# Sparse attention of a decoder trunk: query blocks 0 and 1 become one unit, and VectorE adds the causal mask in PSUM

## Chip, cores and metric

The kernel runs on one core of a Trainium2 chip, in one launch. The metric is the device time of one execution in microseconds (us), lower is better. Engines are named as in the profile: PE (TensorE matmuls), PEld (its weight loads), DVE (VectorE), ACT (ScalarE), POOL (GpSimd), SP (SyncE).

## What is computed

Two layers of a decoder trunk on 512 tokens of width 1024. Each layer runs two token mixers on the same normalised input, stick-breaking attention and native sparse attention (NSA), multiplies each by a SiLU path, projects both up, merges them by sigmoid gates, projects once more and adds the input. The change is in the NSA part:

```python
def masked_softmax(s, mask):
    return jax.nn.softmax(jnp.where(mask, s.astype(jnp.float32), NEG_INF), axis=-1)
...
        ss = jnp.einsum('bgrqd,bgqkd->bgrqk', qb, ks) * scale
        ps = masked_softmax(ss, (tok <= tq[:, None])[:, :, None])
        o_s = jnp.einsum('bgrqk,bgqkd->bgrqd', ps.astype(vs.dtype), vs)
...
        sw = jnp.einsum('bgrqd,bgkd->bgrqk', qb, kw) * scale
        pw = masked_softmax(sw, mw)
        o_w = jnp.einsum('bgrqk,bgkd->bgrqd', pw.astype(vw.dtype), vw)
```

There are 8 query heads in 2 key groups. With 512 tokens, 8 selected blocks of 64 and a window of 512, the selected branch and the window branch both attend to all earlier tokens, so both reduce to causal attention over key blocks of 128 tokens, with different keys and values. Query block i (0 to 3) attends to key blocks 0 to i, and only its last key block needs the triangular mask.

## The kernel before

**Stages of a layer.** Stage X does the stick-breaking attention (lines 1101 to 1185), stage Y the NSA attention (lines 1186 to 1218), and then come the gates, the up projection and the output projection (from line 1220). All large products are float32 split into a high and a low part of a rounded format, three products each (`gemm`, line 436): a projection of 128 columns is 24 matmuls of 512 columns into a bank of tag `acc`, of which there are two.

**Order of the work.** The order of PE's instructions is that of the Python code (line 75). The queues of DVE, ACT and POOL are filled by the framework, by priority and program order, and each engine then runs its queue in order. PE's order is paced by a planner, the class `Pacer` (line 304): every matmul adds its planned time to a clock (0.216 us for 512 columns). Projections wait in a list as filler, and `pump(us)` issues filler matmuls until the clock has moved on by so much, or the filler is empty. So a latency of other engines is covered with projections. In stage Y the filler is what is left of the query projections, then the SiLU paths `z` and the first 13 of 16 gate projections `g` (`Y_FILL`, line 523); what the loop doesn't use is issued by `pc.drain()` (line 1218).

**Stage Y.** For each of 4 head pairs j (one head from each key group g) and each query block i there is a unit u, 16 in all, and each does these steps:

- `nsa_qk` (line 1024): scores into PSUM banks of tag `S` (four banks), at most two key blocks to a bank, both branches t side by side. For each bank and g there is a product with the low part of the keys, kN2, on 64 rows of the array (the two g on different halves), and one with the stacked high parts, kN1, on 128 rows. Units 0 and 1 have one bank for each g, units 2 and 3 have two. Then line 1047 adds the mask of the last key block by a bfloat16 product of `mk_n` with the identity, 256 columns, once for each g.
- Softmax: DVE takes the maximum of each bank (line 1052; over two banks also line 1054), ACT the exponentials with their sums (line 1057), DVE the reciprocal times the branch's gate (lines 1061 and 1062) and the scaling of the probabilities `pr` (line 1065). `pr` has tag `P`, five buffers, two of them for a unit; the SiLU paths use the same tag.
- `nsa_t` (line 1068): four transposes for each key block into the one bank of tag `tp`, a copy by ACT (line 1078), and a pump of `Y_GAP` = 1.5.
- `nsa_pv` (line 1083): 8 products of 128 columns for each key block, on 64 columns of the array, into the bank `o`.

The loop (lines 1193 to 1217) is software-pipelined: `pump(ready - now)`, the products `nsa_pv` of unit u-1, then `nsa_qk` of unit u+1, which sets `ready` to the clock plus `Y_LAT` of that unit, then `nsa_t` of unit u. With a head pair's first unit come `cmp_t` and `cmp_pv` of the compressed branch, whose scores `cmp_qk` (line 980) makes in the pair before (for the first pair, just ahead of the loop):

```python
                    pc.pump(ready - pc.now)
...
                        nsa_pv(o, pTs, (u - 1) % NT)
...
                        pr[u + 1] = nsa_qk(j2, (u + 1) % NT)
                        ready = pc.now + Y_LAT[(u + 1) % NT]
...
                    pTs = nsa_t(pr.pop(u), i, Y_GAP)
```

Of the kernel before, what the change touches and what calls it, by code (L numbers as in the profile page):

```python
# [13 lines left out]
F32 = mybir.dt.float32  # L14
F32R = mybir.dt.float32r
BF16 = mybir.dt.bfloat16
I32 = mybir.dt.int32
AF = mybir.ActivationFunctionType
ALU = mybir.AluOpType
AX = mybir.AxisListType  # L20
PSUM = bass.MemoryType.PSUM

P = 128
# [3 lines left out]
NT = S // P  # L27
# [8 lines left out]
NEG = -1e30  # L36
# [7 lines left out]
X_GAP = (3.5, 3.4)  # L44
Y_GAP = 1.5
F_GAP = ((6.0, 8.0), (5.0, 7.0))
Y_LAT = (7.3, 6.9, 6.9, 8.8)
N_GATE = 13


# [1 line left out]
def kernel(  # L52
# [20 lines left out]
    V, A, T, G = nc.vector, nc.scalar, nc.tensor, nc.gpsimd  # L73

    ctx.enter_context(tc.manual_schedule(engines={mybir.EngineType.PE}))
    cp = ctx.enter_context(tc.tile_pool(name="cp", bufs=1))
# [5 lines left out]
    wk = ctx.enter_context(tc.tile_pool(name="wk", bufs=6))  # L82
# [9 lines left out]
    def s_bank():  # L92
        return bank("S", 4)
# [15 lines left out]
                            bass.AP(tensor=positions.tensor, offset=positions.offset, ap=[[16, NCMP], [1, 32]]))  # L109
    identf = cp.tile([P, P], F32, name="identf")  # L110
    make_identity(nc, identf)
    identb = cp.tile([P, P], BF16, name="identb")
    V.tensor_copy(identb, identf)
    onesf = cp.tile([P, P], F32, name="onesf")
    V.memset(onesf, 1.0)
    eps_t = cp.tile([P, 1], F32, name="eps_t")
# [33 lines left out]
    lns, exps, sigs = deque(maxlen=10), deque(maxlen=10), deque(maxlen=2)  # L150
# [21 lines left out]
    G.affine_select(scr, onesf, pattern=[[-1, P]], compare_op=ALU.is_ge, fill=0.0, base=0, channel_multiplier=1)  # L172
    ntri = cp.tile([P, P], F32R, name="ntri")
    V.tensor_scalar(ntri, scr, -1.0, None, op0=ALU.mult)
    zero = wk.tile([P, P], F32, tag="wk", name="zero")
    V.memset(zero, 0.0)
    mk_sb = cp.tile([P, P], F32, name="mk_sb")
    V.memset(mk_sb, -NEG)
    G.affine_select(mk_sb, mk_sb, pattern=[[1, P]], compare_op=ALU.is_gt, fill=NEG, base=0, channel_multiplier=-1)
    mk_n = cp.tile([P, 2, P], BF16, name="mk_n")  # L180
    mtmp2 = wk.tile([P, P], F32, tag="wk", name="mtmp2")
    G.affine_select(mtmp2, zero, pattern=[[-1, P]], compare_op=ALU.is_ge, fill=NEG, base=0, channel_multiplier=1)
    for b in range(2):
        V.tensor_copy(mk_n[:, b], mtmp2)
    mk_c = cp.tile([P, NT, 32], F32, name="mk_c")
    V.memset(mk_c, 0.0)
    for i in range(NT):
# [159 lines left out]
    pc = Pacer()  # L347

    def mm(out, lhsT, rhs, start, stop, us, **kw):
        T.matmul(out, lhsT, rhs, start=start, stop=stop, **kw)  # L350
        pc.tick(us)

    def tr(out, in_, ident):
        T.transpose(out, in_, ident)  # L354
        pc.tick(0.11)
# [287 lines left out]
    for l in range(depth):  # L643
# [3 lines left out]
        with ExitStack() as lc:  # L647
# [370 lines left out]
                       skip_group_check=True)  # L1018
                return o

            def n_halves(i):
                return [(0, min(2, i + 1))] + ([(2, i + 1)] if i > 1 else [])

            def nsa_qk(j, i):
                nX = n_in[j]
                qs = slice(i * P, (i + 1) * P)
                nk = i + 1
                halves = n_halves(i)
                nh = len(halves)
                pr = [py.tile([P, NT, 2, P], F32, tag="P", name="pr", bufs=5) for _ in range(2)]  # L1030
                mx = py.tile([P, 2, 2, 2], F32, tag="mx", name="mx", bufs=3)
                dn = py.tile([P, 2, 2, 2], F32, tag="dn", name="dn", bufs=3)
                rc = py.tile([P, 2, 2], F32, tag="rc", name="rc", bufs=3)
                sb = [[s_bank() for _ in halves] for _ in range(2)]
                for hf, (a, b) in enumerate(halves):
                    w = (b - a) * 256
                    for g in range(2):
                        gs = slice(g * HD, (g + 1) * HD)
                        mm(sb[g][hf][:, :w], nX[gs, g, qs], kN2[gs, a:b].rearrange("p k t c -> p (k t c)"),
                           True, False, w * .00022)  # L1040
                for hf, (a, b) in enumerate(halves):
                    w = (b - a) * 256
                    for g in range(2):
                        mm(sb[g][hf][:, :w], nX[:, g, qs], kN1[g][:, a:b].rearrange("p k t c -> p (k t c)"),
                           False, b < nk, w * .00043)
                for g in range(2):
                    mm(sb[g][-1][:, w - 256:w], identb, mk_n.rearrange("p t c -> p (t c)"), False, True, 0.11)
                for g in range(2):
                    sbk = []
                    for hf, (a, b) in enumerate(halves):  # L1050
                        sbk.append(sb[g][hf][:, :(b - a) * 256].rearrange("p (k t c) -> p t k c", t=2, c=P))
                        V.tensor_reduce(mx[:, hf, g], sbk[-1], axis=AX.XY, op=ALU.max, negate=True)  # L1052
                    if nh == 2:
                        V.tensor_tensor(mx[:, 0, g], mx[:, 0, g], mx[:, 1, g], op=ALU.min)
                    for hf, (a, b) in enumerate(halves):
                        for t in range(2):
                            exps.append(A.activation(pr[g][:, a:b, t], sbk[hf][:, t], AF.Exp,  # L1057
                                                     bias=mx[:, 0, g, t:t + 1], accum_out=dn[:, hf, g, t:t + 1]))
                    if nh == 2:
                        V.tensor_add(dn[:, 0, g], dn[:, 0, g], dn[:, 1, g])  # L1060
                    V.reciprocal(rc[:, g], dn[:, 0, g])
                    V.tensor_mul(rc[:, g], rc[:, g],
                                 vN[:, i, 264:280].rearrange("p (t g r) -> p t g r", t=2, g=2)[:, :, g, j])
                    for t in range(2):
                        V.tensor_scalar(pr[g][:, :nk, t], pr[g][:, :nk, t], rc[:, g, t:t + 1], None, op0=ALU.mult)  # L1065
                return pr

            def nsa_t(pr, i, gap):
                pTs = []
                for kb in range(i + 1):  # L1070
                    pt = t_bank()
                    ptv = pt.rearrange("p (g t q) -> p g t q", g=2, t=2)
                    for g in range(2):
                        for t in range(2):
                            tr(ptv[:, g, t], pr[g][:, kb, t], identf)
                    pT = py.tile([P, 2, 2, P], F32, tag="pT", name="pT", bufs=NT)
                    with tc.high_priority(offset=PRIO_SB):
                        A.activation(pT.rearrange("p g t q -> p (g t q)"), pt, AF.Copy)  # L1078
                    pTs.append(pT)
                    pc.pump(gap)  # L1080
                return pTs

            def nsa_pv(o, pTs, i):
                qs = slice(i * P, (i + 1) * P)
                for kb, pT in enumerate(pTs):
                    for t in range(2):
                        for g in range(2):
                            mm(o[g * HD:(g + 1) * HD, qs], vN[:, kb, t * P + g * HD:t * P + (g + 1) * HD],
                               pT[:, g, t], False, kb == i and t == 1, 0.115, skip_group_check=True)
# [96 lines left out]
            with ExitStack() as ly:  # L1186
                py = ly.enter_context(tc.tile_pool(name=f"py{l}", bufs=1, reuse_waits="tile"))
                pc.fill.extend([fills[kind](a) for kind, a in Y_FILL])
                sc = cmp_qk(0)
                pr = {0: nsa_qk(0, 0)}  # L1190
                ready = pc.now + Y_LAT[0]
                o, pTs = None, None
                for u in range(17):
                    j, i = u // NT, u % NT
                    pc.pump(ready - pc.now)
                    if i == 0 and u < 16:
                        pcT = cmp_t(sc)
                    if u > 0:
                        nsa_pv(o, pTs, (u - 1) % NT)
                        if i == 0:  # L1200
                            nsa_o(j - 1, o)
                    if u == 16:
                        break
                    if u < 15:
                        j2 = (u + 1) // NT
                        pc.until(lambda: j2 in n_in)
                        pr[u + 1] = nsa_qk(j2, (u + 1) % NT)
                        ready = pc.now + Y_LAT[(u + 1) % NT]
                        if i == 2 and j < 2:
                            pc.until(lambda: ("q", j + 2) in done)  # L1210
                            set_nX(j + 2, n_q[j + 2])
                    pTs = nsa_t(pr.pop(u), i, Y_GAP)
                    if i == 0:
                        o = cmp_pv(pcT)
                    if i == 2 and j < 3:
                        pc.until(lambda: j + 1 in n_in)
                        sc = cmp_qk(j + 1)
                pc.drain()
# [109 lines left out]
```

## Time and profile before

| what | value |
|---|---|
| median of 3 runs | 1007.01 us (1006.08 to 1008.62) |
| the profiled execution's own time | 1005.86 us |
| its span, first to last instruction | 1004.1 us |
| granted PE clock, mean of the span | 0.997 of full speed |
| PE, PEld, DVE, ACT busy | 97%, 77%, 68%, 47% |
| stage Y, layer 0 and layer 1 | about 218 to 408 us, about 701 to 890 us |

How to read it: matmuls are pipelined, and one that lasts 0.39 us can start 0.23 us after the one before it. So what a matmul costs PE is read from start to start in the timeline, not from its duration. In the timeline, a line is a run of like instructions: start, length, engine, line of the code, output and inputs, shapes, count, and in brackets the idle time before it and what ended that. L350 and L354 are the helpers `mm` and `tr`, so PE's work is told apart by its tiles.

### The profile page before, as it was taken

To read this page: it belongs to the slowest core of one execution; us is meant where nothing else is said; L and a number is where in the kernel's file an instruction comes from. 1 tells how busy PE (TensorE), PEld (TensorE's weight loads), DVE (VectorE), ACT (ScalarE), POOL (GpSimd) and SP (SyncE) were. 2 spreads that over 40 slices of the span, in tenths; PEclk is the share of its full clock that TensorE was granted. 3 is DMA by queue.
4 is the path that set the end of the run, shared out by engine and by line. 5 is a ranking of instruction groups with operands and counts; after the bars stand their busy time and mean duration, and the time that the engine had idled before them with its cause. 6 is when DMAs were issued, how large, how long until landed. Compare 5 with 4: busy or idle time off the path is not lost.

```text
span 1004.1 us, 14937 instructions
## 1 busy us (share of the span) xinstructions
PE 974.6 (97%) x5379; PEld 768.9 (77%) x5379; DVE 682.9 (68%) x1337; ACT 467.4 (47%) x1139; POOL 210.1 (21%) x256
## 2 busy tenths in 40 slices
PE   6999999989999999999999999999999999999998
PEld 5776767766878787888888787686777777788886
DVE  6778758778676865566565985587976677655631
ACT  5656356554453443533343545565453443445321
POOL 5153235431110111000012532443210110100000
PEclk9999999999999999999999999999999999999999
DMA  8433246423122222243643224363222221224341
GB/s 281 118 91 100 60 124 156 100 64 74 43 64 52 64 54 64 85 141 93 194 124 95 84 80 122 102 144 93 69 64 54 53 65 49 74 67 141 90 116 53
DMA packets 167530, 94.36 MB, mean 94 GB/s; under 512 B 39568, under 2 KB 160672, under 8 KB 167456
## 3 DMA queue, kind: packets, MB, share of 16 engines
q1 hardware_dynamic: 163120, 88.14, 32.5%
q10 hardware_dynamic: 3632, 3.17, 1.3%
q0 software_dynamic: 704, 2.11, 0.5%
q8 instruction: 42, 0.69, 0.3%
q14 instruction: 32, 0.26, 0.1%
HBM read 80.81 MB, written 6.29 MB: 87 GB/s over the span
## 4 chain that ended last, share of the span: by engine, by line
PE 67%; DVE 6%; issue 2%; ACT 2%; POOL 0%; DMA 0%; SPq 0%; DVEq 0%; ACTq 0%; POOLq 0%
PE acc L350 42%; PE S L350 15%; PE o L350 5%; PE tp L354 4%; PE tp L350 1%; DVE f_t L696 1%; DVE wlo L409 1%; ACT e L220 1%; DVE sp L928 0%; POOL whi L163 0%; DVE sq L500 0%; ACT e L910 0%; DVE sX L510 0%; PE S L354 0%; DVE sK L832 0%
## 5 line engine op out<-in xcount | busy, mean ns | idle before, releaser
L350 PE MATMUL acc<-hh,whi 128*128 128x512 f32 x640 | 257.5, 402 | 0.0
L350 PE MATMUL acc<-hl,whi 128*128 128x512 f32 x640 | 254.6, 399 | 1.2 <-DVE hl L595 1.2
L350 PE MATMUL acc<-hh,wlo 128*128 128x512 f32 x640 | 179.5, 403 | 0.0
L163 POOL TENSOR_SCALAR whi<-raw 128x1024 fp32r<-128x1024 f32 (+1 forms) x84 | 95.5, 1136 | 395.1 <-PE acc L350 323.7
L409 DVE TENSOR_TENSOR wlo<-raw,whi 128x1024 fp32r<-128x1024 f32 (+1 forms) x124 | 154.9, 1249 | 31.6 <-POOL whi L163 21.6
L350 PEld LDWEIGHTS acc<-hh,whi 128*128 128x128 f32 x640 | 120.9, 189 | 26.7 <-issue 2.8
L350 PEld LDWEIGHTS acc<-hl,whi 128*128 128x128 f32 x640 | 120.5, 188 | 25.8 <-DVE hl L595 1.8
L350 PEld LDWEIGHTS acc<-hh,wlo 128*128 128x128 f32 x640 | 118.2, 189 | 26.8 <-issue 3.2
L1078 ACT ACTIVATE pT<-tp 128x512 f32<-128x512 f32 x80 | 48.0, 600 | 132.5 <-PE tp L354 132.0
L409 ACT CAST whi<-raw 128x1024 fp32r<-128x1024 f32 x40 | 42.0, 1050 | 119.8 <-PE S L350 42.4
L1057 ACT ACTIVATE pr<-S,mx 128x256 f32<-128x256 f32 (+1 forms) x192 | 81.8, 447 | 13.7 <-DVE mx L1052 8.1
L1052 DVE TENSOR_REDUCE mx<-S 128x2 f32<-128x512 f32 (+1 forms) x96 | 52.8, 592 | 15.4 <-PE S L350 15.3
L220 ACT ACTIVATE e<-S 128x128 f32<-128x128 f32 (+3 forms) x64 | 25.3, 435 | 80.8 <-DVE S L908 76.7
L350 PE MATMUL acc<-whi,hh 128*128 128x256 f32 (+1 forms) x192 | 57.6, 300 | 3.5 <-DVE gv L664 3.4
L350 PE MATMUL acc<-wlo,hh 128*128 128x256 f32 (+1 forms) x192 | 55.4, 289 | 0.0
L350 PE MATMUL acc<-whi,hl 128*128 128x256 f32 (+1 forms) x192 | 55.3, 288 | 0.0
L1065 DVE TENSOR_SCALAR pr<-pr,rc 128x128 f32<-128x128 f32 (+3 forms) x128 | 51.4, 444 | 1.4
L354 PE MATMUL tp<-identf,pr 128*128 128x128 f32 x320 | 48.7, 274 | 2.4 <-DVE pr L1065 2.3
L350 PE MATMUL S<-yh,wlo 128*128 128x512 f32 x128 | 50.8, 396 | 0.0
L350 PE MATMUL S<-yh,whi 128*128 128x512 f32 x128 | 50.7, 396 | 0.0
L350 PE MATMUL S<-yl,whi 128*128 128x512 f32 x128 | 50.1, 392 | 0.0
L354 PEld LDWEIGHTS tp<-identf,pr 128*128 128x128 f32 x320 | 38.6, 140 | 10.7 <-DVE pr L1065 2.8
(319 smaller groups left out, 1775.6 us busy)
## 6 DMA issues: line engine op xcount, KB each, us to landing
raw<-in_w_in_dram SPq DMA_DIRECT2D x72, 512.0 KB, 3.8
raw<-in_w_in_dram SPq DMA_DIRECT2D x36, 256.0 KB, 3.9
raw<-in_cmp_w_dram SPq DMA_DIRECT2D x16, 512.0 KB, 4.0
raw<-in_w_out_dram SPq DMA_DIRECT2D x16, 512.0 KB, 3.8
raw<-in_w_up_a_dram SPq DMA_DIRECT2D x16, 256.0 KB, 3.1
raw<-in_w_up_b_dram SPq DMA_DIRECT2D x32, 128.0 KB, 3.4
gv<-xs SPq DMA_DIRECT2D x16, 256.0 KB, 2.7
sq<-xq SPq DMA_DIRECT2D x48, 64.0 KB, 2.0
```

The lines of the kernel that those rows point to most:

```text
L163: G.tensor_scalar(dst, src, 1.0, 0.0, op0=ALU.mult, op1=ALU.add)
L220: ins = A.activation(dst, src, func, **kw)
L350: T.matmul(out, lhsT, rhs, start=start, stop=stop, **kw)
L354: T.transpose(out, in_, ident)
L409: for ins in (eng.copy(hi, rv), V.tensor_sub(lo, rv, hi.bitcast(F32))):
L696: V.tensor_tensor(f_v[hf][t * HD:(t + 1) * HD, :, a, g, 0:NCMP], src[:, :, t, hf:hf + NCMP], pe_v[:, hf * 8:(hf + 1) * 8, t:t + 1].to_broa ...
L1052: V.tensor_reduce(mx[:, hf, g], sbk[-1], axis=AX.XY, op=ALU.max, negate=True)
L1057: exps.append(A.activation(pr[g][:, a:b, t], sbk[hf][:, t], AF.Exp, bias=mx[:, 0, g, t:t + 1], accum_out=dn[:, hf, g, t:t + 1]))
L1065: V.tensor_scalar(pr[g][:, :nk, t], pr[g][:, :nk, t], rc[:, g, t:t + 1], None, op0=ALU.mult)
L1078: A.activation(pT.rearrange("p g t q -> p (g t q)"), pt, AF.Copy)
```

## The change

Units 0 and 1 of a head pair become one unit (`UNITS`), whose scores lie in "segments", one bank each: two key blocks of query block 1, then the one of query block 0. So a head pair has three units, of three, three and four key blocks, and the loop runs 13 times, not 17. Each segment of the joint unit has its own softmax (`one` is false). The bfloat16 mask product is gone; instead DVE adds a float32 `mk_n` to the 256 masked columns in PSUM ahead of the maximum. `Y_LAT` gets a value for each of the three units. In the setup, the bfloat16 identity, a zeroed tile and two casts go, and one memset comes.

```diff
-Y_LAT = (7.3, 6.9, 6.9, 8.8)
+Y_LAT = (9.8, 9.2, 10.2)
+UNITS = ((0, 1), (2,), (3,))
...
-    identb = cp.tile([P, P], BF16, name="identb")
-    V.tensor_copy(identb, identf)
...
-    zero = wk.tile([P, P], F32, tag="wk", name="zero")
-    V.memset(zero, 0.0)
...
-    mk_n = cp.tile([P, 2, P], BF16, name="mk_n")
-    mtmp2 = wk.tile([P, P], F32, tag="wk", name="mtmp2")
-    G.affine_select(mtmp2, zero, pattern=[[-1, P]], compare_op=ALU.is_ge, fill=NEG, base=0, channel_multiplier=1)
-    for b in range(2):
-        V.tensor_copy(mk_n[:, b], mtmp2)
+    mk_n = cp.tile([P, P], F32, name="mk_n")
+    V.memset(mk_n, 0.0)
+    G.affine_select(mk_n, mk_n, pattern=[[-1, P]], compare_op=ALU.is_ge, fill=NEG, base=0, channel_multiplier=1)
...
+            def nsa_blocks(un):
+                return [(i, kb) for i in reversed(un) for kb in range(i + 1)]
+
+            def nsa_qk(j, un):
                 nX = n_in[j]
...
+                segs, at_slot = [], 0
+                for i in reversed(un):
+                    for a in range(0, i + 1, 2):
+                        b = min(a + 2, i + 1)
+                        segs.append((i, a, b, at_slot))
+                        at_slot += b - a
+                one = len(un) == 1
...
+                sb = [[s_bank()[:, :(b - a) * 256] for _, a, b, _ in segs] for _ in range(2)]
...
-                    mm(sb[g][-1][:, w - 256:w], identb, mk_n.rearrange("p t c -> p (t c)"), False, True, 0.11)
...
+                    for n, (i, a, b, _) in enumerate(segs):
+                        if b == i + 1:
+                            dg = sb[g][n][:, (b - a - 1) * 256:].rearrange("p (t c) -> p t c", t=2)
+                            V.tensor_tensor(dg, dg, mk_n[:, None, :].to_broadcast([P, 2, P]), op=ALU.add)
+                        V.tensor_reduce(mx[:, n, g], sb[g][n].rearrange("p (k t c) -> p t k c", t=2, c=P), axis=AX.XY,
+                                        op=ALU.max, negate=True)
+                    if one:
                         V.tensor_tensor(mx[:, 0, g], mx[:, 0, g], mx[:, 1, g], op=ALU.min)
...
+                    for n, (i, a, b, o) in enumerate(segs[:1] if one else segs):
+                        V.reciprocal(rc[:, n, g], dn[:, n, g])
+                        V.tensor_mul(rc[:, n, g], rc[:, n, g], gate[:, i, :, g, j])
+                        e = at_slot if one else o + b - a
+                        for t in range(2):
+                            V.tensor_scalar(pr[g][:, o:e, t], pr[g][:, o:e, t], rc[:, n, g, t:t + 1], None, op0=ALU.mult)
                 return pr
...
-                for u in range(17):
-                    j, i = u // NT, u % NT
+                for u in range(4 * NU + 1):
+                    j, v = u // NU, u % NU
                     pc.pump(ready - pc.now)
-                    if i == 0 and u < 16:
+                    if v == 0 and j < 4:
                         pcT = cmp_t(sc)
                     if u > 0:
-                        nsa_pv(o, pTs, (u - 1) % NT)
-                        if i == 0:
+                        nsa_pv(o, pTs, UNITS[(u - 1) % NU])
+                        if v == 0:
                             nsa_o(j - 1, o)
...
+                        pr[u + 1] = nsa_qk(j2, UNITS[v2])
+                        ready = pc.now + Y_LAT[v2]
+                        if v == 1 and j < 2:
...
+                    pTs = nsa_t(pr.pop(u), UNITS[v], Y_GAP)
```

## Rows read from the trace of the kernel before

**Rows 1.** Page: the span, and PE's busy time with its share and instructions.
```profile
span 1004.1 us, 14937 instructions
PE 974.6 (97%) x5379; PEld 768.9 (77%) x5379; DVE 682.9 (68%) x1337; ACT 467.4 (47%) x1139; POOL 210.1 (21%) x256
```
**Rows 2.** Windows, stage Y: busy us (instructions) of PE, PEld, DVE, ACT, POOL; clock; DMA.
```profile
218.00:262.00 44.00, 41.87 (x243) 32.70 (x244) 39.86 (x92) 22.58 (x69) 8.05 (x7) 1.00 0.27 67
262.00:306.00 44.00, 43.97 (x291) 34.65 (x289) 31.39 (x77) 19.37 (x64) 4.24 (x4) 1.00 0.22 54
394.00:440.00 46.00, 46.00 (x230) 37.54 (x229) 22.73 (x30) 23.79 (x37) 1.05 (x1) 1.00 0.35 98
701.00:745.00 44.00, 42.41 (x245) 32.51 (x244) 41.38 (x95) 23.35 (x70) 8.27 (x7) 1.00 0.29 73
```
**Rows 3.** Waits of PE in 217 to 440 (first row) and 700 to 870.
```profile
PE tp L354 <- DVE pr L1065: 2.1, 1, 2.1
...
PE tp L354 <- DVE sc L1002: 1.4, 1, 1.4
PE tp L354 <- DVE pr L1065: 0.2, 1, 0.2
```
**Rows 4.** Timeline of PE, layer 0, second head pair: start us, length us.
```profile
262.40 0.82 PE L350 MATMUL S<-kN,nX 64*128 64x256 f32 x4
...
263.29 0.60 PE L354 MATMUL tp<-identf,pr 128*128 128x128 f32 x4
...
271.84 1.97 PE L350 MATMUL o<-pT,vN 128*64 128x128 f32 x32
273.74 1.17 PE L350 MATMUL S<-kN,nX 64*128 64x512 f32 x4
...
274.98 0.60 PE L354 MATMUL tp<-identf,pr 128*128 128x128 f32 x4
...
280.24 2.02 PE L350 MATMUL acc<-hh,wlo 128*128 128x512 f32 x8
282.10 0.40 PE L350 MATMUL acc<-hh,whi 128*128 128x512 f32 x1
282.43 0.66 PE L350 MATMUL o<-pT,vN 128*64 128x128 f32 x8
283.01 1.51 PE L350 MATMUL S<-kN,nX 64*128 64x512 f32 x8
284.37 0.39 PE L350 MATMUL S<-mk_n,identb 128*128 128x256 bf16 x2
284.60 0.60 PE L354 MATMUL tp<-identf,pr 128*128 128x128 f32 x4
...
292.02 1.09 PE L350 MATMUL o<-pT,vN 128*64 128x128 f32 x16
293.05 1.86 PE L350 MATMUL S<-kN,nX 64*128 64x512 f32 x8
...
294.98 0.60 PE L354 MATMUL tp<-identf,pr 128*128 128x128 f32 x4
...
304.80 1.53 PE L350 MATMUL o<-pT,vN 128*64 128x128 f32 x24
306.26 0.82 PE L350 MATMUL S<-kN,nX 64*128 64x256 f32 x4
```
**Rows 5.** Timeline of DVE, same head pair: the last scaling of its unit 3.
```profile
305.32 0.87 DVE L1065 TENSOR_SCALAR pr<-pr,rc 128x512 f32<-128x512 f32 x2
```
**Rows 6.** Timeline of DVE, layer 0, first head pair.
```profile
218.89 0.42 DVE L992 TENSOR_TENSOR sc<-tp,mk_c 128x256 f32<-128x256 f32 x1 [0.72 <-PE tp L350]
219.23 0.74 DVE L492 SCALAR_TENSOR_TENSOR xq<-xq,cols,yy 128x512 f32<-128x512 f32 x1
...
231.22 0.47 DVE L1065 TENSOR_SCALAR pr<-pr,rc 128x128 f32<-128x128 f32 x2
...
232.28 1.27 DVE L1052 TENSOR_REDUCE mx<-S 128x2 f32<-128x512 f32 x2
```

More of the change, by code (lines that the diff above doesn't have):

```diff
@@ L1019, in cmp_pv @@
                 return o
-            def n_halves(i):
-                return [(0, min(2, i + 1))] + ([(2, i + 1)] if i > 1 else [])
-            def nsa_qk(j, i):
+            def nsa_blocks(un):
+                return [(i, kb) for i in reversed(un) for kb in range(i + 1)]
+            def nsa_qk(j, un):
                 nX = n_in[j]
[L1026 to L1029, printed above, removed]
+                segs, at_slot = [], 0
[5 more added lines that the diff above has]
+                one = len(un) == 1
                 pr = [py.tile([P, NT, 2, P], F32, tag="P", name="pr", bufs=5) for _ in range(2)]
@@ L1032, in nsa_qk @@
                 dn = py.tile([P, 2, 2, 2], F32, tag="dn", name="dn", bufs=3)
[L1033 to L1036, printed above, removed]
+                rc = py.tile([P, 2, 2, 2], F32, tag="rc", name="rc", bufs=3)
+                sb = [[s_bank()[:, :(b - a) * 256] for _, a, b, _ in segs] for _ in range(2)]
+                for n, (i, a, b, _) in enumerate(segs):
@@ L1037, in nsa_qk @@
                     for g in range(2):
                         gs = slice(g * HD, (g + 1) * HD)
[L1039 to L1042, printed above, removed]
+                        mm(sb[g][n], nX[gs, g, i * P:(i + 1) * P], kN2[gs, a:b].rearrange("p k t c -> p (k t c)"),
+                           True, False, (b - a) * 256 * .00022)
@@ L1043, in nsa_qk @@
+                for n, (i, a, b, _) in enumerate(segs):
                     for g in range(2):
-                        mm(sb[g][hf][:, :w], nX[:, g, qs], kN1[g][:, a:b].rearrange("p k t c -> p (k t c)"),
-                           False, b < nk, w * .00043)
+                        mm(sb[g][n], nX[:, g, i * P:(i + 1) * P], kN1[g][:, a:b].rearrange("p k t c -> p (k t c)"),
+                           False, True, (b - a) * 256 * .00043)
+                gate = vN[:, :, 264:280].rearrange("p i (t g r) -> p i t g r", t=2, g=2)
@@ L1046, in nsa_qk @@
                 for g in range(2):
-                    mm(sb[g][-1][:, w - 256:w], identb, mk_n.rearrange("p t c -> p (t c)"), False, True, 0.11)
[L1048 to L1053, printed above, removed]
+                    for n, (i, a, b, _) in enumerate(segs):
+                        if b == i + 1:
[3 more added lines that the diff above has]
+                                        op=ALU.max, negate=True)
@@ L1054, in nsa_qk @@
+                    if one:
                         V.tensor_tensor(mx[:, 0, g], mx[:, 0, g], mx[:, 1, g], op=ALU.min)
-                    for hf, (a, b) in enumerate(halves):
+                    for n, (i, a, b, o) in enumerate(segs):
+                        sv = sb[g][n].rearrange("p (k t c) -> p t k c", t=2, c=P)
                         for t in range(2):
-                            exps.append(A.activation(pr[g][:, a:b, t], sbk[hf][:, t], AF.Exp,
-                                                     bias=mx[:, 0, g, t:t + 1], accum_out=dn[:, hf, g, t:t + 1]))
@@ L1059, in nsa_qk @@
-                    if nh == 2:
+                            exps.append(A.activation(pr[g][:, o:o + b - a, t], sv[:, t], AF.Exp,
+                                                     bias=mx[:, 0 if one else n, g, t:t + 1],
+                                                     accum_out=dn[:, n, g, t:t + 1]))
+                    if one:
                         V.tensor_add(dn[:, 0, g], dn[:, 0, g], dn[:, 1, g])
-                    V.reciprocal(rc[:, g], dn[:, 0, g])
-                    V.tensor_mul(rc[:, g], rc[:, g],
-                                 vN[:, i, 264:280].rearrange("p (t g r) -> p t g r", t=2, g=2)[:, :, g, j])
@@ L1064, in nsa_qk @@
-                    for t in range(2):
-                        V.tensor_scalar(pr[g][:, :nk, t], pr[g][:, :nk, t], rc[:, g, t:t + 1], None, op0=ALU.mult)
+                    for n, (i, a, b, o) in enumerate(segs[:1] if one else segs):
[4 more added lines that the diff above has]
+                            V.tensor_scalar(pr[g][:, o:e, t], pr[g][:, o:e, t], rc[:, n, g, t:t + 1], None, op0=ALU.mult)
@@ L1066, in nsa_qk, with nsa_t @@
                 return pr
-            def nsa_t(pr, i, gap):
+            def nsa_t(pr, un, gap):
                 pTs = []
-                for kb in range(i + 1):
+                for slot in range(len(nsa_blocks(un))):
                     pt = t_bank()
@@ L1074, in nsa_t @@
                         for t in range(2):
-                            tr(ptv[:, g, t], pr[g][:, kb, t], identf)
+                            tr(ptv[:, g, t], pr[g][:, slot, t], identf)
                     pT = py.tile([P, 2, 2, P], F32, tag="pT", name="pT", bufs=NT)
@@ L1081, in nsa_t, with nsa_pv @@
                 return pTs
-            def nsa_pv(o, pTs, i):
-                qs = slice(i * P, (i + 1) * P)
-                for kb, pT in enumerate(pTs):
+            def nsa_pv(o, pTs, un):
+                for (i, kb), pT in zip(nsa_blocks(un), pTs):
+                    qs = slice(i * P, (i + 1) * P)
                     for t in range(2):
@@ L1189 @@
                 sc = cmp_qk(0)
-                pr = {0: nsa_qk(0, 0)}
+                NU = len(UNITS)
+                pr = {0: nsa_qk(0, UNITS[0])}
                 ready = pc.now + Y_LAT[0]
                 o, pTs = None, None
-                for u in range(17):
-                    j, i = u // NT, u % NT
+                for u in range(4 * NU + 1):
+                    j, v = u // NU, u % NU
                     pc.pump(ready - pc.now)
-                    if i == 0 and u < 16:
+                    if v == 0 and j < 4:
                         pcT = cmp_t(sc)
                     if u > 0:
-                        nsa_pv(o, pTs, (u - 1) % NT)
-                        if i == 0:
+                        nsa_pv(o, pTs, UNITS[(u - 1) % NU])
+                        if v == 0:
                             nsa_o(j - 1, o)
-                    if u == 16:
+                    if j == 4:
                         break
-                    if u < 15:
-                        j2 = (u + 1) // NT
+                    if u + 1 < 4 * NU:
+                        j2, v2 = (u + 1) // NU, (u + 1) % NU
                         pc.until(lambda: j2 in n_in)
-                        pr[u + 1] = nsa_qk(j2, (u + 1) % NT)
-                        ready = pc.now + Y_LAT[(u + 1) % NT]
-                        if i == 2 and j < 2:
+                        pr[u + 1] = nsa_qk(j2, UNITS[v2])
+                        ready = pc.now + Y_LAT[v2]
+                        if v == 1 and j < 2:
                             pc.until(lambda: ("q", j + 2) in done)
                             set_nX(j + 2, n_q[j + 2])
-                    pTs = nsa_t(pr.pop(u), i, Y_GAP)
-                    if i == 0:
+                    pTs = nsa_t(pr.pop(u), UNITS[v], Y_GAP)
+                    if v == 0:
                         o = cmp_pv(pcT)
-                    if i == 2 and j < 3:
+                    if v == 1 and j < 3:
                         pc.until(lambda: j + 1 in n_in)
```

## The prediction

> **What bounds the kernel now.** I read the page first. PE is busy for 974.6 of 1004.1 us, and no other engine for more than 68% [rows 1]. A share over the whole span mixes stages, so next come the windows of stage Y, where the change lies. In the second head pair PE is busy for 43.97 of 44 us and DVE for 31.39, while in the first pair DVE is busy for 39.86 of 44 in layer 0 and for 41.38 in layer 1, and there PE has 2.1 and 1.6 us idle [rows 2]. Third, the waits of PE in the two stages: three and no more, together 3.7 us, all in the first pairs and all for DVE's results [rows 3]. So PE is the bound of stage Y, except at its start. Behind the loop PE goes on without a hole, 46.00 of 46 us [rows 2], so a microsecond of PE work less in the loop should be a microsecond less in the end.
>
> The Trainium skill speaks against that: "Perfetto Trace Analysis", section "Identifying the Most-Contended Engine", says that matmul busy time is a bad measure of how full TensorE is, and that the share of weight loads is a better one. By it PE would be a fifth free here. I go by the starts: eight filler matmuls and the one behind them start 1.86 us apart [rows 4], 0.2325 us each, and PE idles nowhere in this pair.
>
> **What PE loses: the mask product.** Two of them, from their start to the next instruction, take 284.37 to 284.60 = 0.23 us [rows 4]. Each of the 4 units of a pair has two, and there are 4 pairs in 2 layers: 0.23 x 4 x 8 = 7.4 us. All of it is on PE's path.
>
> **The joint unit.** From the first score product to the next instruction unit 0 takes 0.89 us, unit 1 1.24, unit 2 1.59, unit 3 1.93 [rows 4]. The joint unit has the shapes of unit 2 (for each g a bank of 512 columns and one of 256). Without masks that is 1.36, unit 2 itself 1.36, unit 3 1.70, in all 4.42 us against 5.65: 1.23 a pair, x8 = 9.8 us, of which 7.4 are the masks and 2.4 the second change-over between half-height and full-height products. `nsa_pv` behaves alike: 8 products take 0.58 us, 16 take 1.03, 24 take 1.46 [rows 4], so one run of 24 saves 0.15 a pair, 1.2 us. The step into such a run takes 0.33 us (282.10 to 282.43) where the filler's is 0.2325, 0.10 x 8 = 0.8 us. The transposes, `cmp_t`, `cmp_pv`, `cmp_qk` and the filler keep their counts. **Off PE: 9.8 + 1.2 + 0.8 = 11.8 us.**
>
> **The filler lasts.** By the planner's constants, with 0.216 a matmul, the loop pumps 34 filler matmuls before the first unit, 113 a pair and 4 more in the last: 490. After the change these are 46, 109 a pair, 4 more and 10 fewer at the end: 476. So it isn't exhausted sooner, and what is left over is drained behind the loop.
>
> **What DVE gains: the mask additions.** Two for each unit and g of query blocks, 8 a pair, 64 in all, of 128x256 in PSUM. The trace has none of just this kind. The nearest row adds the compressed mask to 256 columns from PSUM: 0.42 us long, the next one starting 0.34 after it [rows 6]. As a lower bound I take nothing (where DVE is idle the work costs the end nothing), as an upper one half the step of the 512-column reductions with all their length, 1.27 / 2 = 0.64 us [rows 6]. I take 0.34: 2.7 us a pair. In the second pair DVE goes from 31.4 to 34.1 us; a pair gets shorter by about 2, so it is at about 81%. PE covers that, as long as the probabilities come in time.
>
> **Are they in time?** The planner's clock runs behind by 0.2325 / 0.216 = 1.08. Before, from the end of a unit's scores to its first transpose, unit 2 has 284.60 to 294.98 = 10.4 us. Unit 3 has 294.98 to 307.15 (306.26 + 0.89) = 12.2, and its last scaling ends at 306.19 [rows 5], so it uses 11.2 of 12.2: little slack, but no wait. After: `Y_LAT` x 1.08, plus the products of the unit before (1.90 for four blocks, 1.46 for three), plus the next scores. The joint unit gets 10.5 + 0.3 (`cmp_t`, half of a run of four transposes, 0.60 [rows 4]) + 1.9 + 1.4 = 14.1 us, unit 2 9.9 + 1.5 + 1.7 = 13.1, unit 3 11.0 + 1.5 + 1.4 = 13.9. Two additions make unit 3 use 11.9 of 13.9. The joint unit has the DVE work of two small units and four additions (1.4 us). In steady state I cost this at nothing; the cover is 2 us of slack, and without it each late microsecond is one of PE's.
>
> **The start of stage Y.** Here DVE is late already. In layer 0 it ends the scaling of unit 0 at 231.7 [rows 6] and PE waits 2.1 us for it; in layer 1 PE waits 1.4 and 0.2 [rows 3]. After, PE comes later: 12 filler matmuls more (2.8 us), 0.5 for the joint scores, 0.1 for the next, 3.4 in all. DVE has more to do before the first transposes: four additions (1.4), two reductions (1.27), four more scalings (about 1.0 by 0.47 for two), their small reciprocals and products (0.6), less the 0.47 of the last key block, which is wanted one or two pumps later: about 3.8. More filler also brings more DVE work with it. I take 1.0 us more waiting in each layer, 2 in all. Bounds: all 3.7 us of waiting go, or 3 us come in each layer, which is every one of the additions and reductions waited for.
>
> **The setup.** A cast of the identity, a memset and two casts go and a memset comes, some tenths of a microsecond while x is being loaded. I take nothing, 0.5 either way.
>
> **Sum.** -11.8 + 2.0 = -9.8 us. The profiled execution took 1005.86 us (span 1004.1 and 1.8 around it), so it would take 996.1; the median of the runs shown lies 1.1 above it, so 997.2. Its own range: 1007.0 - 11.8 - 3.7 - 0.5 = 991.0 to 1007.0 - 11.8 + 6 + 0.5 = 1001.7.
>
> **Rivals.**
> First, **DVE becomes the bound in the first head pair and takes the gain back.** DVE's 39.9 and 41.4 us there plus 2.7 make 42.6 and 44.1, in a pair that PE could do in about 42. If all three units of these pairs are late by 1.5 us in both layers, that is 9 us in place of 2: 1007.0 - 11.8 + 9 = 1004.2. For it: PE's only waits are here [rows 3]. Against it: later units have 13 to 14 us, and work put off may spill into the second pair, which has room. Chance 0.10.
> Second, **PE has room, and what leaves it leaves holes.** This is the skill's rule above made into a mechanism: weight loads fill 34.65 of 44 us [rows 2], the rest is slack, the loop's length is set elsewhere, and the time stays at 1007. Against it: PE's starts, and no other engine is nearly full in the second pair. Chance 0.03.
> Third, **slower: the additions lengthen each unit's chain past its cover.** Place: the wait of the first transpose for the scaling, line 1065, in all 24 units. It decides from about 13.1 us of chain on; before, unit 3 uses 11.2. The joint unit writes both its probability tiles from the same five buffers that the SiLU paths use, so its second tile can be held until the unit before has been transposed, and all four additions stand ahead of its first exponentials. With 1 us of wait in each of 24 units: 1007.0 - 11.8 + 24 = 1019. Against it: the 2 us of slack worked out above. Chance 0.06.
>
> **Numbers.** A measurement of this kernel can tell about 0.3%, 3 us, from no change. The forecast has 0.81, and all of its own range is faster by more than that. The first and the second rival are within 0.3%, 0.13; slower 0.06. The range is the forecast's, its lower end drawn in a little, because all waits would have to vanish for it, and its upper end set at the first rival's time: 992 to 1004.5.
>
> **What would show it.** In the profile after: PE's score products of a pair in three runs of about 1.36, 1.36 and 1.70 us and no bfloat16 product; 24 runs of `nsa_pv` where there are 32; 64 additions on DVE of 0.3 to 0.4 us; PE's waits in stage Y still in the first pairs alone, 4 to 8 us together; PE busy about 12 us less. I'd be wrong if PE waits for the scaled probabilities in later pairs, if the additions take 0.6 us, or if a stage outside Y changes by more than a microsecond.

## The result, and the profile after

The changed kernel takes 1003.2 us (median of 5 runs, 998.69 to 1003.34), against 1007.64 us for the kernel before in runs beside it (5, 1006.08 to 1009.37): a ratio of 0.9948 with a 95% interval of 0.9934 to 0.9963, by which it is 5.2 us less (the two medians lie 4.4 apart). A later series gave 1002.15 us, ratio 0.9951 (0.9938 to 0.9964). The forecast was 997.2 in a range of 992 to 1004.5: the sign and the range held, but only about half of the 9.8 us worked out came.

The page of the changed kernel: span, engines, and PE's granted clock in 40 slices.

```profile
span 1001.5 us, 14850 instructions
...
PE 967.7 (97%) x5315; PEld 769.1 (77%) x5315; DVE 701.9 (70%) x1398; ACT 467.3 (47%) x1139; POOL 208.9 (21%) x256
...
PEclk9999999898999999999999999999899999999999
```

PE is busy for 6.9 us less than in [rows 1], DVE for 19. The clock has three slices at 8; the first of them lies ahead of stage Y. Next the windows of stage Y, columns as in [rows 2]: the first head pair, the second one, the first pair of layer 1, then two short stretches.

```profile
218.00:262.00 44.00, 41.53 (x210) 32.55 (x209) 40.60 (x96) 22.36 (x68) 6.75 (x6) 0.92 0.24 61
262.00:303.00 41.00, 41.00 (x272) 33.43 (x271) 32.15 (x86) 18.98 (x63) 5.25 (x5) 1.00 0.25 64
701.00:745.00 44.00, 39.70 (x200) 31.19 (x201) 40.76 (x99) 21.60 (x67) 7.13 (x7) 0.92 0.23 58
234.67:241.50 6.83, 6.33 (x19) 5.13 (x20) 4.65 (x13) 2.32 (x6) 1.27 (x1) 0.50 0.16 38
715.95:722.78 6.83, 5.83 (x17) 4.63 (x18) 4.72 (x14) 2.69 (x6) 1.29 (x1) 0.50 0.17 41
```

The second pair is close to the forecast: PE is busy for 41.00 of 41 us, the pair takes 41.1 us where it took 43.9, DVE is at 78%. In both first pairs PE is granted 0.92 on the mean, and the last two rows show why: for 6.83 us in each layer the clock is at 0.50, the lower of its two levels (1.2 GHz, not 2.4). PE's waits in the two stages, as [rows 3]:

```profile
PE S L345 <- ACT pr L1055: 2.5, 2, 1.8
...
PE S L345 <- ACT pr L1055: 4.3, 2, 2.6
```

They are of a new kind. PE no longer waits at the transposes for scaled probabilities, but at score products (tile S) for the exponentials (line 1055 here). PE's timeline of layer 0 there:

```profile
231.51 0.38 PE L349 MATMUL tp<-identf,sc 128*128 128x128 f32 x2
231.81 0.49 PE L345 MATMUL S<-kN,nX 64*128 64x512 f32 x2
234.12 0.38 PE L345 MATMUL S<-kN,nX 64*128 64x256 f32 x1 [1.81 <-ACT pr L1055]
235.17 2.15 PE L345 MATMUL S<-kN,nX 64*128 64x256 f32 x5 [0.66 <-ACT pr L1055]
237.12 1.06 PE L349 MATMUL tp<-identf,pr 128*128 128x128 f32 x4
237.83 2.91 PE L345 MATMUL acc<-hh,wlo 128*128 128x512 f32 x6
240.53 0.63 PE L345 MATMUL acc<-hh,whi 128*128 128x512 f32 x1
240.96 0.87 PE L349 MATMUL tp<-identf,pr 128*128 128x128 f32 x4
241.58 0.48 PE L345 MATMUL acc<-hl,whi 128*128 128x512 f32 x1
```

These are the scores of the second unit. Two products find a free bank at once, the other two banks are waited for one after the other. The half clock covers the last five score products and what follows: six filler matmuls from 237.83 to 240.53 are 0.45 us apart, not 0.2325. From `cmp_t` to the first transposes it takes 237.12 - 231.51 = 5.6 us where 1.7 are work (0.3 and 1.36), and from there to 241.58 it takes 4.5 us where 2.4 are at full clock (235.59 to 238.00 in the run with a busy wait, below): 3.9 + 2.1 = 6.0 us lost. In layer 1 the same (711.45, 718.90, 723.12) gives 5.8 + 1.8 = 7.6. Before, 2.3 and 1.9 us were lost there by the starts.

The loss has two parts of about the same size. PE's idle times are 2.5 and 4.3 us, where they were 2.1 and 1.6. Most of the rest is the clock: PE is busy for 6.33 and 5.83 us at half speed, where a matmul takes 0.45 us and not 0.2325, so about half of that time, 3.2 and 2.9 us, is an estimate of what the clock costs. It explains within about 1 us why PE is busy for only 6.9 us less in all, though 11.8 us of work left it.

Why the exponentials are late: ACT's timeline, then DVE's, both of layer 0.

```profile
233.05 0.47 ACT L1055 ACTIVATE pr<-S,mx 128x256 f32<-128x256 f32 x1 [4.55 <-DVE mx L1048]
...
234.66 0.36 ACT L1055 ACTIVATE pr<-S,mx 128x128 f32<-128x128 f32 x1
```

```profile
228.53 1.22 DVE L404 TENSOR_TENSOR wlo<-raw,whi 128x1024 fp32r<-128x1024 f32 x1
...
230.81 0.42 DVE L1047 TENSOR_TENSOR S<-S,mk_n 128x256 f32<-128x256 f32 x1
231.14 1.28 DVE L1065 TENSOR_SCALAR pr<-pr,rc 128x128 f32<-128x128 f32 x2
232.34 0.68 DVE L1048 TENSOR_REDUCE mx<-S 128x2 f32<-128x512 f32 x1
232.94 0.42 DVE L1047 TENSOR_TENSOR S<-S,mk_n 128x256 f32<-128x256 f32 x1
...
233.86 0.41 DVE L1048 TENSOR_REDUCE mx<-S 128x2 f32<-128x256 f32 x1
```

The joint unit's scores were done at 220.9. But the mask additions and maxima of its second key group come 10 to 13 us later, behind the norms, the compressed branch, the split of a weight tile (line 404) and part of the first group's own scalings in DVE's full queue. ACT had been idle for 4.55 us. And as the joint unit has two banks for each group, it holds all four; the next scores must wait until its last exponential has read.

**The balance of the profiled executions.** From the first score product to the first product of the up projection, layer 0 takes 203.1 us (219.55 to 422.68) where it took 205.5 (218.78 to 424.30), layer 1 204.5 (699.58 to 904.09) where it took 205.4 (701.33 to 906.76): -3.3. PE's work less by 5.9 a layer, plus the losses of 6.0 and 7.6 in place of 2.3 and 1.9, gives -2.4; the two agree within 1 us. (The two profiled executions lie only 2.7 us apart, 1005.86 and 1003.20 us: that of the kernel before was one of its faster ones.) Ahead of stage Y the changed kernel is 0.8 us late: between 172 and 190 us its granted clock is 0.81, where the kernel before has 0.91, with PE busy for 15.41 us in both. No row ties that to the change: the changed kernel itself has 0.91 there in its second profile.

### The profile page after: what moved, and what is told of

It reads as the page before. It is cut to its first block, busy times and chain, and to the rows that moved or that the text cites. A ratio compares the mean times of both kernels' runs of the same rounds, so it can differ in the third digit from the quotient of the medians.

```text
span 1001.5 us, 14850 instructions
## 1 busy us (share of the span) xinstructions
PE 967.7 (97%) x5315; PEld 769.1 (77%) x5315; DVE 701.9 (70%) x1398; ACT 467.3 (47%) x1139; POOL 208.9 (21%) x256
## 4 chain that ended last, share of the span: by engine, by line
PE 76%; DVE 13%; ACT 6%; issue 3%; DMA 1%; POOL 1%; SPq 0%; ACTq 0%; DVEq 0%; POOLq 0%
PE acc L345 48%; PE S L345 16%; PE o L345 6%; PE tp L349 4%; DVE f_t L691 2%; DVE wlo L404 2%; PE tp L345 2%; ACT e L215 1%; ACT e L905 1%; DVE sX L505 1%; DVE hl L590 1%; DVE spl L923 1%; DVE sp L923 1%; DMA x_sb<-in_x_dram 1%; DVE e L907 1%
## 5 line engine op out<-in xcount | busy, mean ns | idle before, releaser
L345 PE MATMUL acc<-hh,wlo 128*128 128x512 f32 x640 | 181.7, 408 | 0.0
L1055 ACT ACTIVATE pr<-S,mx 128x256 f32<-128x256 f32 x192 | 81.9, 446 | 17.4 <-DVE mx L1048 10.3
L1048 DVE TENSOR_REDUCE mx<-S 128x2 f32<-128x512 f32 (+1 forms) x96 | 55.3, 593 | 11.8 <-PE S L345 11.7
L1065 DVE TENSOR_SCALAR pr<-pr,rc 128x128 f32<-128x128 f32 (+3 forms) x128 | 55.0, 471 | 1.1
L345 PE MATMUL S<-kN,nX 64*128 64x512 f32 (+1 forms) x192 | 42.2, 407 | 6.8 <-ACT pr L1055 6.8
```

The costliest lines, as they stand in the source:

```text
L1048: V.tensor_reduce(mx[:, n, g], sb[g][n].rearrange("p (k t c) -> p t k c", t=2, c=P), axis=AX.XY, op=ALU.max, negate=True)
L1055: exps.append(A.activation(pr[g][:, o:o + b - a, t], sv[:, t], AF.Exp, bias=mx[:, 0 if one else n, g, t:t + 1], accum_out=dn[:, n, g, t:t ...
L1065: V.tensor_scalar(pr[g][:, o:e, t], pr[g][:, o:e, t], rc[:, n, g, t:t + 1], None, op0=ALU.mult)
```

## The experiments

All times are medians; a ratio is to the kernel before in runs beside it. Theory A blames the score banks that the joint unit holds, theory B a VectorE that is full whatever its order, theory C the additions alone.

**Each half alone.** The joint units with the product mask kept (below, left out: the setup of before), and the additions in the 16 units of before.

```diff
+                           False, b < i + 1, (b - a) * 256 * .00043)
+                for n, (i, a, b, _) in enumerate(segs):
+                    if b == i + 1:
+                        for g in range(2):
+                            mm(sb[g][n][:, (b - a - 1) * 256:], identb, mk_n.rearrange("p t c -> p (t c)"), False, True, 0.11)
...
-                            V.tensor_tensor(dg, dg, mk_n[:, None, :].to_broadcast([P, 2, P]), op=ALU.add)
```

> The joint units alone: the mask is added by the bfloat16 product again, VectorE adds nothing. PE gets 7.4 us back. Theory A: the second unit's scores still wait for the last exponential of the joint unit, which comes at most 1.4 us sooner (four additions), so 2 to 4 us a layer are still lost: 1004 to 1008 us. Theory C (the additions are what makes the joint unit late): the waits at the start go, 1003.2 + 7.4 - 12 = about 998 us.

Measured: 1007.56 us, ratio 1.0003 (0.9993 to 1.0012), by its time on theory A's side. But its waits (layer 0, then layer 1) are not theory A's:

```profile
PE tp L355 <- ACT pT L1085: 1.9, 2, 1.6
PE S L351 <- ACT pr L1062: 0.2, 1, 0.2
...
PE tp L355 <- DVE pr L1072: 2.8, 2, 1.9
PE tp L355 <- ACT pT L1085: 0.4, 1, 0.4
```

The wait for score banks is down to 0.2 us: without the additions the last exponentials are in time, as theory C has it. PE waits at transposes instead, for 5.1 us. The 4.4 us that left PE (11.8 less the 7.4 of the masks) are lost again: 1.6 us more of waits than before, some 1.8 by the clock (an estimate: its mean is 0.96 over the 44 us of layer 1's first pair), and about 1 us that isn't accounted for.

```diff
-                for g in range(2):
-                    mm(sb[g][-1][:, w - 256:w], identb, mk_n.rearrange("p t c -> p (t c)"), False, True, 0.11)
...
+                        if b == nk:
+                            dg = sb[g][hf][:, (b - a - 1) * 256:(b - a) * 256].rearrange("p (t c) -> p t c", t=2)
+                            V.tensor_tensor(dg, dg, mk_n[:, None, :].to_broadcast([P, 2, P]), op=ALU.add)
```

> The additions alone: 16 units and the waits planned as in the kernel before, the mask added by VectorE. PE loses 7.4 us of products. Theory A: unit 0 holds two of four banks, so no scores wait; PE waits for late probabilities in the first pair as before, 0 to 1 us more a layer: 1000 to 1002 us. Theory C: 64 additions make the first pair late by more than 2 us a layer in the same way, 1004 us or more.

Measured: 1005.07 us, ratio 0.9987 (0.9976 to 0.9998), 3 us above theory A's range and on theory C's side. Its waits, layer 0 first:

```profile
PE tp L348 <- DVE sc L996: 2.0, 1, 2.0
PE tp L348 <- DVE pr L1060: 1.3, 2, 0.8
...
PE tp L348 <- DVE pr L1060: 2.0, 2, 1.2
PE tp L348 <- DVE sc L996: 1.4, 1, 1.4
```

No score waits for a bank, as theory A has it, but 6.7 us of waits for DVE are left where there were 3.7. So the new wait for score banks needs both halves: four banks held, and additions that make their last reader late. But each half alone loses most of its gain in the first pairs, too; here 3.0 us go into waits and an estimated 1.8 into the clock, whose mean is 0.96 over the 44 us of layer 0's first pair.

**More filler ahead of the first unit.** One number in the changed kernel: 15.0, 12.5 or 11.0 in place of 9.8.

```diff
-                ready = pc.now + Y_LAT[0]
+                ready = pc.now + 15.0
```

> One number: the wait ahead of the first unit of stage Y is planned as 15.0, not 9.8, so 24 more filler matmuls (5.6 us) stand ahead of the scores of the second unit; the work is the same. Theory A (the joint unit holds all four score banks, so the second unit's scores wait for its last exponential; PE idles for microseconds and its clock falls): nothing waits any more and the clock stays at full speed in stage Y, so the 5.6 us lost in layer 0 and 7.5 us in layer 1 beside the undisturbed order come back, about 990 to 992 us. Theory B (VectorE is simply full in the first head pair, and the loss only moves): PE waits for about 4 us a layer later in the first pair, 999 us or more.

> The changed kernel with the wait ahead of the first unit planned as 12.5, about half way from 9.8 to 15.0, no priority. The last exponential of the joint unit ended 14.2 us (layer 0) and 16.0 us (layer 1) after its scores; 12.5 planned covers some 13.4 us and the transposes of the compressed branch. If the second unit's scores then wait 1 us in layer 0 and 2 to 3 us in layer 1, and the clock falls in layer 1 alone: 997 to 1000 us. If the clock falls in neither, 995 to 997 us.

> The changed kernel with the wait ahead of the first unit planned as 11.0, not 9.8 (six filler matmuls more), no priority. With 12.5 nothing waits for score banks and the clock stays. If the wait for the banks shrinks in step, by 1.3 us, 1.7 us stay in layer 0 and 3.5 us in layer 1: the clock falls in layer 1 alone, 998 to 1000 us. If the clock still falls in both layers: 1000 to 1001.5 us. If VectorE's queue comes out so that nothing waits, as with 12.5: 995 to 997 us.

Measured: 996.59 us with 15.0, ratio 0.9893 (0.9880 to 0.9906); 996.0 with 12.5, ratio 0.9894 (0.9877 to 0.9910); 998.72 with 11.0, ratio 0.9921 (0.9908 to 0.9933). The waits with 12.5, layer 0 first:

```profile
PE acc L345 <- DVE zt L862: 1.1, 1, 1.1
PE tp L349 <- DVE pr L1065: 0.2, 1, 0.2
...
PE acc L345 <- DVE zt L862: 1.7, 1, 1.7
PE S L345 <- ACT pr L1055: 1.6, 1, 1.6
```

The clock stays at 1.00 in both first pairs with 12.5 and 15.0. With 11.0 the waits for banks are 1.3 and 3.2 us, and the clock still falls in both layers of the profiled execution, which at 1000.67 us was the slowest of the five. The expectation for 11.0 overlooked that 12.5 leaves 1.6 us of wait for a bank in layer 1. Theory A's core holds: covered by work that is due anyway, most of the loss goes. Theory B has a part, too: 1.1 and 1.7 us wait behind DVE at the evacuation of a SiLU projection, and 15.0 gave no more than 12.5 and some 5 us less than expected. All three versions beat the changed kernel and the kernel before.

**The same for the kernel before.** Its first wait at 10.0 in place of 7.3.

> The kernel before, with the wait ahead of its first unit planned as 10.0 in place of 7.3 (13 filler matmuls more), nothing else. Its waits in the first pairs, 2.3 and 1.9 us by the starts, are covered too: 1007.3 - 4 = about 1003 us. Then the change is worth 7 us where both have their start covered (996 with 12.5), and some 4 of the 11 us between the kernel before and that one come from the longer start alone. If those waits only move, as VectorE is full: 1006 to 1007 us.

Measured: 1002.62 us, ratio 0.9959 (0.9946 to 0.9971), as expected; PE's waits in stage Y are down to 0.4 us. This one number brings the kernel before to about 1 us from the changed kernel. With the start covered in both, the change is worth 0.9894 / 0.9959, or 6.6 us (by the two intervals some 4 to 9). The 11.8 that leave PE in both layers, less the 4.2 us of waits more that the version with 12.5 has (1.1, 0.2, 1.7 and 1.6 against 0.4), give 7.6, within 1 us of it.

**A busy wait.** Products that nobody reads, where PE idled:

```diff
                         pcT = cmp_t(sc)
+                        if u == 0:
+                            hot = o_bank()
+                            for _ in range(6 if l else 4):
+                                T.matmul(hot, onesf, r_bc, start=True, stop=True)
```

> The changed kernel, with 4 (layer 0) and 6 (layer 1) float32 products of 512 columns that nobody reads, into the bank o, ahead of the second unit's scores: PE is busy where it waited, and what it waits for is as late as before. If the fall of the clock behind the wait costs time of its own, the clock stays at full speed in stage Y and the time is 3 to 5 us below the changed kernel's, about 998 to 1000 us. If only the wait costs, the time stays at 1003 us.

Measured: 1000.77 us, ratio 0.9939 (0.9927 to 0.9951). The granted clock is 1.00 in both first pairs, and 0.996 to 0.998 over the span in all five runs, so it is PE's idling that lets it fall. The gain against the changed kernel is 1.4 to 2.4 us, less than expected, and the timeline of PE shows what gave some of it back:

```profile
230.49 0.38 PE L349 MATMUL tp<-identf,sc 128*128 128x128 f32 x2
230.71 3.60 PE L1202 MATMUL o<-r_bc,onesf 128*128 128x512 f32 x8
234.23 1.52 PE L345 MATMUL S<-kN,nX 64*128 64x512 f32 x8
235.59 0.60 PE L349 MATMUL tp<-identf,pr 128*128 128x128 f32 x4
...
238.00 0.47 PE L345 MATMUL acc<-hl,whi 128*128 128x512 f32 x1
...
255.09 0.66 PE L349 MATMUL tp<-identf,pr 128*128 128x128 f32 x4 [2.10 <-ACT pT L1078]
```

The second unit's scores follow the idle products (each is two records) without a wait, at full clock. From `cmp_t` to the filler behind the second transposes it takes 238.00 - 230.49 = 7.5 us, 2.6 less than in the changed kernel; in layer 1 it takes 9.2 us, 2.4 less. Then PE, faster, meets the next late result at 255.09 and waits 2.1 us there, and 0.4 in layer 1: 2.5 of the 5.0 us are left.

**The first softmax at a higher priority.** The softmax of head pair 0's joint unit comes earlier in the queues, in two forms: above the two additions that read the compressed scores out of the bank `tp` (offset `PRIO_SB`, 600), or below them (200). The first form also with the first wait at 12.0, the second also with 12.5.

```diff
+                soon = ExitStack()
+                if j == 0 and len(un) == 2:
+                    soon.enter_context(tc.high_priority(offset=PRIO_SB))
+                with soon:
```

> The changed kernel with the softmax of the first joint unit of each layer (lines 1043 to 1065 for head pair 0, unit 0) at a priority that moves its additions, maxima and scalings ahead of the query norms in VectorE's queue; PE's order and all waits planned are unchanged. Theory A2 (what is late is the order of VectorE's queue: the second key group's additions stand behind the norms and the scalings of the first): the joint unit's last exponential comes some 5 us sooner, the second unit's scores wait for nothing, the clock stays at full speed: 994 to 997 us. Theory B (VectorE is full, the loss only moves): the norms and the compressed branch are late instead, PE waits 3 us or more a layer in the first pair for them: 1000 us or more.

> The same, and the wait ahead of the first unit is planned as 12.0 in place of 9.8 (11 filler matmuls more ahead of the second unit's scores). Theory A2: 1 to 2 us less than with the priority alone, since the compressed branch's softmax, which now comes later, is covered too: 993 to 996 us. Theory B: no better than the priority alone.

> As the run with the first joint unit's softmax moved ahead, but at a priority below that of the two additions that read the compressed scores out of the one bank tp, so these stay in front; wait planned as 9.8. In the earlier run PE waited 3.7 and 2.1 us for that bank; this should be gone. Theory A2 (order alone): all else is in time, 996 us. Theory B (VectorE is full): now the compressed branch's softmax is late for its transposes, PE waits about 2 us there in each layer and the clock may fall: 1000 to 1004 us.

> The same with the wait ahead of the first unit planned as 12.5. Theory B with its cover: the compressed branch is in time as well, about 994 to 996 us, no more than 2 us better than 12.5 without a priority (996.0), since 1.2 and 1.85 us of wait for a projection's evacuation are all that is left there.

Measured, in this order: 1007.05 us, ratio 0.9996 (0.9987 to 1.0005); with 12.0 1000.47, ratio 0.9931 (0.9918 to 0.9944); the second form 1008.83, ratio 1.0022 (1.0013 to 1.0031); with 12.5 1005.51, ratio 0.9988 (0.9980 to 0.9997). The waits of the first of them, layer 0, and of the third, layer 0; then a window of the changed kernel, its first 15 us of stage Y:

```profile
PE tp L345 <- DVE sc L988: 3.5, 1, 3.5
PE tp L349 <- DVE sc L997: 1.9, 1, 1.9
```

```profile
PE tp L349 <- DVE sc L997: 7.0, 1, 7.0
```

```profile
219.50:234.50 15.00, 13.19 (x59) 9.77 (x58) 14.74 (x36) 6.89 (x22) 3.39 (x3) 1.00 0.26 57
```

Theory A2 falls. What is put in front is in time, and what it displaces is late: the bank `tp`, then the compressed branch's softmax (line 997), by more than I had allowed. DVE is busy for 14.74 of these 15 us, and in both orders tried something that PE needs was late. That no order would do is not shown. Theory B didn't do well either: with 12.0 the first form gained 6.6 us, where it expected nothing, and with 12.5 the second form missed the 994 to 996 us by 9.5. None of the four came near the 996.0 of 12.5 without a priority.

**The changed kernel once more.**

> The changed kernel once more, on the same chip as the others. Its runs gave 1002.6 to 1003.3 us four times and 998.7 once, with the mean granted clock at 0.989 and 0.995. Expected: 1003 us where the clock falls in both layers' first pairs, 998 to 1000 where it doesn't.

Measured: 1002.15 us (1000.64 to 1003.87). Five of the six runs have a mean clock of 0.989 to 0.991 and take 1001.8 us or more; the one at 0.995 takes 1000.64. In the first series the four at 0.989 take 1002.57 to 1003.34 and the one at 0.995 takes 998.69. So the mean clock differs from run to run, and most of the spread goes with it. The profile of this series shows it in layer 0 (a window, then PE's score products):

```profile
218.00:262.00 44.00, 41.52 (x213) 32.33 (x213) 41.59 (x99) 22.65 (x69) 6.86 (x6) 0.96 0.26 64
```

```profile
234.68 0.38 PE L345 MATMUL S<-kN,nX 64*128 64x256 f32 x1 [1.81 <-ACT pr L1055]
235.73 1.94 PE L345 MATMUL S<-kN,nX 64*128 64x256 f32 x5 [0.67 <-ACT pr L1055]
```

The program and its two waits are the same as in the first profile (1.81 and 0.66 us), but the mean clock of the pair is 0.96, not 0.92, and from `cmp_t` to the filler behind the second transposes it takes 8.8 us (232.07 to 240.85) in place of 10.1.

## Why the prediction was right, and where it wasn't

- **PE's work: right.** The second pair of the changed kernel, PE's score products and what follows them:

```profile
264.93 1.52 PE L345 MATMUL S<-kN,nX 64*128 64x512 f32 x8
266.28 0.60 PE L349 MATMUL tp<-identf,pr 128*128 128x128 f32 x4
...
279.02 1.52 PE L345 MATMUL S<-kN,nX 64*128 64x512 f32 x8
280.38 0.60 PE L349 MATMUL tp<-identf,pr 128*128 128x128 f32 x4
...
291.80 1.86 PE L345 MATMUL S<-kN,nX 64*128 64x512 f32 x8
293.49 0.60 PE L349 MATMUL tp<-identf,pr 128*128 128x128 f32 x4
...
306.02 1.52 PE L345 MATMUL S<-kN,nX 64*128 64x512 f32 x8
```

  The three runs take 1.35, 1.36 and 1.69 us, where 1.36, 1.36 and 1.70 were worked out from [rows 4]. The sign that PE would be busy for about 12 us less didn't come, for the reason given above: 6.9.
- **The additions: right.** 64 of them, and a step of 0.33 where I took 0.34 (230.81 to 231.14). Their group:

```profile
L1047 DVE TENSOR_TENSOR S<-S,mk_n 128x256 f32<-128x256 f32 x64 | 26.4, 422 | 2.7 <-PE S L345 2.7
```

- **In time in the later pairs: right.** No wait of PE there. The third rival, a chain past its cover in all 24 units, didn't come.
- **"I take 1.0 us more waiting in each layer, 2 in all": this step failed.** By the starts the loss grew by 3.7 and 5.7 us, 9.4 in all. The larger part is a term that the sum doesn't have: PE's clock. Behind the waits it was at its lower level for 6.83 us in each layer, at a cost of about 3 us a layer; I put that at nothing without a reason. The waiting itself grew by 0.4 and 2.7 us, 3.1 in all, which lies within my bounds but at another place and by another mechanism. I looked for it where it was before, at the transposes, and never asked what the second unit's scores need: four score banks that units 0 and 1 used to share out and the joint unit holds alone.
- **The range held by its upper end.** The forecast's own range ended at 1001.7 us, and 1003.2 lies above it. What reached further up was the first rival's time, 1004.2, which was worked out from another mechanism, all three units of the first pairs being late. That the measured time is near it is luck.
- **The first rival, DVE as the bound of the first pair, had the place right.** DVE is busy there for nearly all of the first 15 us, and moving its work about made other things late. But only the second unit waits, and it isn't lost time as such: 2.7 us more planned wait, filled with work that was due later, got about 6 us back (1002.15 to 996.0 in the same series).
- **The second rival, PE with room to spare, is refuted.** In the second pair weight loads fill 33.43 of 41 us, 82% where it was 79%, and the pair got shorter by 2.8 us (262.40 to 306.26 before [rows 4], 264.93 to 306.02 after). Four filler matmuls fewer (109, not 113) are 0.9 of them; the rest covers all of the 1.5 us of work that left PE in a pair. The Trainium skill's rule for judging how full TensorE is ("Perfetto Trace Analysis", "Identifying the Most-Contended Engine") would have misled here; the starts didn't.

Left open: what would make DVE's work at the start of stage Y itself less, whether another order of it would do, and why the clock's fall differs from run to run. None was tried.

## What to carry to other kernels

When two units of work become one, count what the one now holds at once, here the PSUM banks, and ask for each who needs it next and which late reader frees it. On an engine that is otherwise full, price a wait by what it does to the clock as well as by its length. Where a pipeline starts behind a busy helper engine, put work that is due anyway ahead of its first wait, before trying to reorder the helper.

## What was unexpected of the hardware

The clock fell behind waits in which PE was not wholly idle: in layer 0 it was granted 0.50 from 234.67 us on, behind an idle time of 1.81 us and one score product, within a second idle time of 0.66 us. A single wait of 2.1 us in the kernel before [rows 3] had not lowered it. It came back at 241.50, after PE had been issuing products one behind the other from 235.17 on. Nor does the wait alone decide how long the clock stays low: the same kernel with the same two waits had a mean of 0.92 in that pair in one profile and 0.96 in another. The Trainium skill ("TensorE: Matmul & The Clock Gate", section "What's actually happening") says that PE's recent activity sets the clock to one of two levels, and the traces agree: 0.50 behind the wait, 1.00 where the wait was filled with products nobody reads.
